# A hybrid attention and recurrence block on one core: where the position tables, the gate weights and two heads' weights stand in the instruction order

## The chip, the cores and the metric

One core of a Trainium2 chip runs the whole kernel. The time is that of the device for one execution, in microseconds (us): the median of three runs of the kernel before is 1267.96 us (1267.69 to 1269.3). Engines: PE multiplies matrices, DVE does elementwise work and scans, ACT does activations and copies, POOL elementwise work on the side, and SP issues the DMA transfers from one queue, in program order. Every engine carries out its instructions in the order in which they stand; it waits only when an operand is not there or a buffer is not free.

## The reference

The block has 2048 latent tokens of width 1024 and 256 context tokens. Only the parts that the change touches are shown: the biases of the windowed attention (`rpb`), the recurrence (RG-LRU) in two directions, and the heads' projections.

```python
q, k, v, z_a, u, z_l = jnp.split(h @ w, [aw, 2*aw, 3*aw, 4*aw, 4*aw + lw], axis=-1)
k_c, v_c = jnp.split(hc @ w[:, aw:3*aw], 2, axis=-1)
u_c = hc @ w[:, 4*aw:4*aw + lw]
attn = neighbourhood_attention(rope(qn), qn, rope(kn), v, kcn, vch, rpb)   # 8 heads x 64

uc, ucc = depthwise_conv(u, conv_w, conv_b), depthwise_conv(u_c, conv_w, conv_b)
for d, reverse in ((0, False), (1, True)):                 # 8 blocks x 64 channels
    r = sigmoid(u_block @ w_a[d] + b_a[d]); i = sigmoid(u_block @ w_x[d] + b_x[d])
    log_a = -8 * r * softplus(-lam[d])
    a, b = exp(log_a), sqrt(-expm1(2 * log_a)) * (i * u)
    h_t = a_t * h_prev + b_t                               # context first, then latent
y = forward + backward
mix = concat([attn * silu(z_a), y * silu(z_l)]) @ w_out
out = x + gate * mix
```

## The kernel before

Every projection of float32 data is made of three fp16 matmuls (high and low parts of activations and weights, lines 345 to 347 in `proj_ct`). A weight tile is loaded whole into `wraw`, its absolute maximum is found on DVE (L320) and brought to one value by PE and DVE (L112 to L117), and it is split into `wh` on ACT (L325) and `wl` on DVE (L326); this is `wsplit`.

Phase 1 norms the tokens, builds the position tables (`tables`), then projects and convolves the recurrence's input in four chunks of 128 channels (`u_proj(c)`: PE matmuls, an ACT copy `us` L363, DVE convolution L365 and L370). `gate` (L577) sums eight loaded rows of `w_mod` on DVE into `gacc` and closes with two matmuls on PE (L596).

For each chunk c, `lru` loads four 64x2x64 pieces of the recurrence's gate weights into `gw` (L424), after POOL has zeroed it (L421), and splits it on DVE into `gh` (L427) and `gl` (L428). For each direction d it multiplies them with `uh`, `ul` on PE (L448 to L450, called the gate matmuls here), takes tanh on ACT (L452) and works out the coefficients on ACT and DVE (L453 to L460); X is a (128 x 2304) and I its companion. Direction 0 is scanned on DVE at once (L462), direction 1 behind both (L469, three scans of 256, 1024 and 1024 steps); POOL adds the two (L472), and SP writes the chunk's result away. Between the directions `fill(d)` stands: two blocks of the silu gate (`z_units`, 24 matmuls a block, L480 on ACT and L481 on DVE) and, for d = 0, the weights of the next silu group (`z_group`). After chunk 0 and after chunk 1 the code writes `u_proj(2)` and `u_proj(3)`.

Three buffers matter. `gw` is one of two slots of the pool tag "z", which `us` (the convolution's copies) and `sz` (the silu gate's blocks) use as well, so a chunk's `gw` waits for the last `us` in front of it and the next `us` waits for `gw` to be read. Raw weights have one slot in each of two pools. In `tables` the source of constants `ng` stands in SBUF, in the tables' pool.

`tables` copies each quarter's table together on ACT (`te`, L665 to L668), sends it to DRAM (`d_t`), and copies it from there in 24 transfers (L675) and two fills (L677) to `d_e`, from which the attention loads its biases later. All of this is issued on SP.

Phase 2 begins with the weights of heads 0 and 1 (`wsplit`, lines 947 and 948), then `head_proj(0)`: projection (L604 to L606), norms, rotation on POOL (from L707), transposes by DMA and the first attention step. `lru_gate` (L975) loads its first weights `wraw` behind that, to be measured on DVE (L320).

Where the code gives the order only in part, a scheduler sets it: it merges the engines' instructions by its own times, within what buffers, program order of a stream and queues allow.

Of the kernel before, what the change touches and what calls it, by code (L numbers as in the profile page):

```python
# [7 lines left out]
F32 = mybir.dt.float32  # L8
# [51 lines left out]
class K:  # L60
# [351 lines left out]
    def lru(self, c, uc, p, fill):  # L412


        nc, a = self.nc, self.a
        N = CTX + S
        t = lambda x: p.tile([128, N], F32, tag=x, name=x, bufs=2)
        A, X = t("A"), t("X")
        gl = p.tile([128, 4, 128], F32R, tag="gl", name="gl", bufs=1)
        gw = self.zp.tile([128, 512], F32, tag="z", name="gw", bufs=2).rearrange("p (g c) -> p g c", g=4)  # L420
        nc.gpsimd.memset(gw, 0.0)  # L421
        for g, nm in enumerate(("lru_wa", "lru_wx")):
            for f in range(2):
                nc.sync.dma_start(gw[64 * f:64 * f + 64, 2 * g:2 * g + 2, 64 * f:64 * f + 64],  # L424
                                  a[nm][:, 2 * c + f].rearrange("d i j -> i d j"))
        gh = p.tile([128, 4, 128], F32R, tag="gh", name="gh", bufs=1)
        nc.vector.tensor_copy(gh, gw)  # L427
        nc.vector.tensor_tensor(gl, gw, gh.bitcast(F32), ALU.subtract)  # L428

        I = t("I")  # L430
        uh = p.tile([128, N], F32R, tag="uh", name="uh", bufs=1)
        ul = p.tile([128, N], F32R, tag="ul", name="ul", bufs=1)
        done = []
        for d in range(2):
            if d:
                A, X, I = t("A"), t("X"), t("I")
            kc = slice(4 * d + c, 4 * d + c + 1)
            for b in (0, CTX, CTX + 512, CTX + 1024, CTX + 1536):
                m = 512 if b else CTX
                s = slice(b, b + m)  # L440
                u = uc[:, s]
                if d == 0:
                    nc.scalar.copy(uh[:, s], u)  # L443
                    nc.gpsimd.tensor_tensor(ul[:, s], u, uh[:, s].bitcast(F32), ALU.subtract)  # L444
                for g, dst in enumerate((X, I)):
                    w = 2 * g + d
                    q = self.any_bank()[:, :m]
                    nc.tensor.matmul(q, gh[:, w, :], uh[:, s], start=True, stop=False)  # L448
                    nc.tensor.matmul(q, gh[:, w, :], ul[:, s], start=False, stop=False)
                    nc.tensor.matmul(q, gl[:, w, :], uh[:, s], start=False, stop=True)  # L450
                    k = 8 * g + 4 * d + c
                    nc.scalar.activation(dst[:, s], q, AF.Tanh, bias=self.hb[:, k:k + 1], scale=0.5)  # L452
                nc.vector.scalar_tensor_tensor(I[:, s], I[:, s], 1.0, u, ALU.add, ALU.mult)  # L453
            for h in range(2):
                s = slice(N // 2 * h, N // 2 * (h + 1))
                nc.scalar.activation(A[:, s], X[:, s], AF.Exp, bias=self.nk4[:, kc], scale=self.nk4[:, kc])
                nc.vector.scalar_tensor_tensor(I[:, s], A[:, s], 1.0, I[:, s], ALU.add, ALU.mult)
                nc.scalar.activation(X[:, s], X[:, s], AF.Tanh, bias=self.k2[:, kc], scale=self.k2[:, kc])
            nc.scalar.activation(X, X, AF.Sqrt, scale=0.25)
            nc.vector.tensor_tensor(X, X, I, ALU.mult)  # L460
            if d == 0:
                nc.vector.tensor_tensor_scan(A, A, X, 0.0, ALU.mult, ALU.add)  # L462
            done.append(A)
            fill(d)
        F, A = done
        init = 0.0
        for o, m in ((0, CTX), (CTX + S // 2, S // 2), (CTX, S // 2)):
            r = lambda x: x[:, o:o + m][:, ::-1]
            nc.vector.tensor_tensor_scan(r(A), r(A), r(X), init, ALU.mult, ALU.add)  # L469
            init = A[:, o:o + 1]  # L470
            if o:
                nc.gpsimd.tensor_tensor(F[:, o:o + m], A[:, o:o + m], F[:, o:o + m], ALU.add)  # L472
                nc.sync.dma_start(self.d_y[128 * c:128 * c + 128, o - CTX:o - CTX + m], F[:, o:o + m])
# [10 lines left out]
    def phase1(self, left, right):  # L484
# [14 lines left out]
        with ExitStack() as s1:  # L499
# [54 lines left out]
            with ExitStack() as s2:  # L554
                p = self.pool(s2, "lru")
                ug[2] = u_group(2)
                z_group()

                def z_units(c, d):
                    wh, wl, _ = za[c]  # L560
                    for tb in (2 * d, 2 * d + 1):
                        z = self.silu_z(self.zp, self.bank("mm"), wh, wl, self.zs[:, c:c + 1], tb)
                        dz = self.d_z[c][tb].rearrange("p (j f x) -> p f j x", j=4, f=2)
                        for f in range(2):
                            zf = z[:, 256 * f:256 * f + 256]
                            nc.sync.dma_start(dz[:, f, 0:3], zf[:, 32:224].rearrange("p (j x) -> p j x", j=3))
                            nc.sync.dma_start(dz[:, f, 3].rearrange("p (e x) -> p e x", e=2),
                                              bass.AP(zf.tensor, zf.offset, [list(zf.ap[0]), [224, 2], [1, 32]]))
                    if d == 0 and c < 3:
                        z_group()  # L570

                for c in range(4):
                    self.lru(c, ucs[c], p, lambda d, c=c: z_units(c, d))
                    if c < 2:
                        ucs.append(u_proj(c + 2))

# [32 lines left out]
    def tables(self, q):  # L609
# [26 lines left out]
        nc.sync.dma_start(d_r, rp)  # L636
        d_f = self.drm.tile([16, 2, NH, 15, 32], F32, name="d_f")
        ng = q.tile([128, 864], F32, name="ng")
        nc.gpsimd.memset(ng, NEG)
        ff = d_f.rearrange("q t h k c -> (q t h k c)").rearrange("(p n) -> p n", p=128)  # L640
        for i in range(2):
            nc.sync.dma_start(ff[:, 480 * i:480 * i + 480], ng[:, 0:480])
# [7 lines left out]
        for t in range(3):  # L650

            if t != 1:
                src = lambda k0, k1: d_f[:, t // 2, :, k0:k1, :].rearrange("q h k c -> h q (k c)")
                u = q.tile([128, 864], F32, tag="tu", name="tu")
                nc.gpsimd.memset(u, NEG)
                nc.sync.dma_start(u[:, 224:480], src(3, 11))
                w = q.tile([128, 480], F32, tag="tw", name="tw")
                nc.sync.dma_start(w, src(0, 15))
            for r in range(4):
                e = q.tile([128, 1024], F32, tag="te", name="te", bufs=2)  # L660
                for tab, o, g in ((u, 0, 5), (w, 640, 3)):
                    eo = e[:, o:o + 128 * g].rearrange("p (g c r) -> p g c r", c=32, r=4)
                    ti = tab[:, 96 - 32 * r:96 - 32 * r + 128 * g].rearrange("p (g r c) -> p g c r", r=4, c=32)
                    if t == 1:
                        nc.scalar.copy(eo[:, :, 0:16], ti[:, :, 16:32])  # L665
                        nc.scalar.copy(eo[:, :, 16:32], ti[:, :, 0:16])
                    else:
                        nc.scalar.copy(eo, ti)  # L668
                nc.sync.dma_start(d_t[r][t], e)

        self.d_e = [self.drm.tile([2, NH, 64, 3, w], F32, name=f"d_e{i}") for i, w in enumerate(BW)]

        def spread(rt, f, r, o, src, n):
            e = self.d_e[rt][f].rearrange("h (c r) t w -> (h c) r t w", r=4)[:, r, :, o:o + n]
            nc.sync.dma_start(e, d_t[r][:, :, src:src + n].rearrange("t p w -> p t w"))  # L675
        for f, o in ((0, 256), (1, 0)):
            nc.sync.dma_start(self.d_e[2 * f][f].rearrange("h (c r) t w -> (h c) (r t) w", r=4)[:, :, o:o + 128],  # L677
                              ng[:, 0:128].unsqueeze(1).broadcast_to([128, 12, 128]))
        for r in range(4):
            for f in range(2):  # L680
                spread(1, f, r, 0, 128 * (1 - f), 512)
            spread(0, 1, r, 0, 128, 384)
            spread(0, 0, r, 0, 768, 256)
            spread(2, 0, r, 0, 128, 384)
            spread(2, 1, r, 128, 640, 256)

    def bias_load(self, p, h, rt):

# [233 lines left out]
    def phase2(self, left, right):  # L922
# [5 lines left out]
        with ExitStack() as sg:  # L928
# [13 lines left out]
                nc.gpsimd.memset(x[:, :, 64:128], 0.0)  # L942
            self.zero = self.const.tile([128, 1], F32, name="zero")
            nc.gpsimd.memset(self.zero, 0.0)
            self.hw, self.bias, self.o = {}, [], {}
            with self.tc.issue_after(self.last.ins):
                for i in range(2):
                    self.hw[i] = self.wsplit(*self.head_w(i))
                for H in self.head_proj(0, p, q):
                    pass  # L950
            lz = self.lru_gate()
# [191 lines left out]
```

## Time and profile before

| | |
|---|---|
| median of three runs | 1267.96 us (1267.69 to 1269.3) |
| profiled execution | 1268.18 us |
| its span in the trace | 1266.4 us |
| mean granted TensorE clock | 0.945 |
| PE busy | 1116.4 us, 88% of the span |
| DVE, ACT, POOL busy | 926.4, 618.0 and 472.2 us |

A row of the trace gives the start and duration of an instruction, and in brackets the engine's idle time in front of it with what ended it. A matmul's duration overlaps the next one's, so the busy time of a stretch divided by its matmuls gives the pace. Three stretches are to be told apart: the recurrence's chunks (about 120 to 420 us of the span), the handoff to head 0 (to about 480), and the attention behind it.

### The profile page before, as it was taken

How to read it: one execution, taken by the hardware profiler on the slowest of the kernel's cores; microseconds unless marked ns; L12 is line 12 of the kernel's file. 1: busy time of each engine (PE TensorE's matmuls, PEld its weight loads, DVE VectorE, ACT ScalarE, POOL GpSimd, SP SyncE). 2: the span in 40 equal slices, each digit the busy share in tenths (PEclk: the TensorE clock that was granted, in tenths of full speed). 3: DMA queues.
4: the chain of work that ended last, by engine and by line, in shares of the span. 5: the costliest groups of instructions: out<-in, count | busy, mean ns of one | idle time of the engine just before them, and what ended most of it. 6: DMA issues, size and time to landing. Idle time of an engine off the chain costs nothing. (4 is left out here: it accounts for less than half of the span.)

```text
span 1266.4 us, 26204 instructions
## 1 busy us (share of the span) xinstructions
PE 1116.4 (88%) x9964; PEld 854.8 (67%) x9964; DVE 926.4 (73%) x2548; ACT 618.0 (49%) x1189; POOL 472.2 (37%) x861
## 2 busy tenths in 40 slices
PE   7767658996985959999999999999998997999997
PEld 1434324453543857899878988789887876888786
DVE  7898556869688667888978988788888874554432
ACT  1697118283588125655646555555555644231200
POOL 0245100403030377566564655646556462000000
PEclk9798869998998888999989999999999998999999
DMA  9746962111112623344533445335353537436352
GB/s 352 270 165 243 310 193 51 59 46 56 24 30 59 152 35 82 70 104 107 110 83 64 109 92 126 83 66 108 89 122 81 136 93 193 142 101 187 109 153 67
DMA packets 196014, 149.50 MB, mean 118 GB/s; under 512 B 129453, under 2 KB 168109, under 8 KB 195887
## 3 DMA queue, kind: packets, MB, share of 16 engines
q1 hardware_dynamic: 195887, 147.82, 43.6%
q8 instruction: 78, 1.28, 0.4%
q14 instruction: 49, 0.40, 0.1%
HBM read 96.42 MB, written 47.94 MB: 114 GB/s over the span
## 5 line engine op out<-in xcount | busy, mean ns | idle before, releaser
L604 PE MATMUL mm<-wh,hh 128*128 128x192 f16 x960 | 237.0, 247 | 1.7 <-DVE V L762 1.6
L605 PE MATMUL mm<-wl,hh 128*128 128x192 f16 x960 | 236.9, 247 | 0.0
L606 PE MATMUL mm<-wh,hl 128*128 128x192 f16 x960 | 236.9, 247 | 0.0
L895 DVE TENSOR_TENSOR Pl<-pt,Ph 128x384 f16<-128x384 f32 (+1 forms) x256 | 127.9, 517 | 57.2 <-ACT Ph L894 56.4
L345 PE MATMUL mm<-hh,wh 128*128 128x512 f16 x384 | 150.8, 393 | 17.9 <-DVE sz L481 12.0
L346 PE MATMUL mm<-hl,wh 128*128 128x512 f16 x384 | 150.0, 391 | 7.8 <-POOL hl L290 6.9
L887 ACT ACTIVATE SP<-SP,nb 128x640 f32<-128x640 f32 (+1 forms) x128 | 110.4, 880 | 94.2 <-DVE nb L885 89.8
L347 PE MATMUL mm<-hh,wl 128*128 128x512 f16 x384 | 148.7, 388 | 0.7 <-DVE wl L326 0.7
L894 ACT CAST Ph<-pt 128x384 f16<-128x384 f32 (+1 forms) x256 | 107.1, 452 | 79.2 <-PE pt L893 75.3
L893 PE MATMUL pt<-id,SP 128*128 128x128 f32 x704 | 116.9, 283 | 2.4 <-ACT SP L887 1.7
L604 PEld LDWEIGHTS <-hh 128*128 128x128 f16 x1024 | 100.6, 98 | 8.9 <-issue 5.2
L605 PEld LDWEIGHTS <-hh 128*128 128x128 f16 x1024 | 100.6, 98 | 2.8 <-issue 1.6
L606 PEld LDWEIGHTS <-hl 128*128 128x128 f16 x1024 | 100.5, 98 | 0.8
L882 DVE CUSTOM_DVE_ANT_0 SP<-sl,b,m 128x384 f32<-128x384 f32 (+1 forms) x128 | 93.4, 736 | 6.9 <-PE sl L830 6.2
L830 PE MATMUL sl<-qk,qt 128*128 128x128 f16 (+2 forms) x800 | 79.4, 232 | 17.9 <-DMA qk<-ST 8.2
L444 POOL TENSOR_TENSOR ul<-uc,uh 128x512 fp32r<-128x512 f32 (+1 forms) x20 | 30.5, 1553 | 151.0 <-ACT uh L443 150.9
L900 PEld LDWEIGHTS <-Ph 128*128 128x128 f16 x1408 | 79.5, 97 | 9.0 <-ACT Ph L894 2.9
L893 PEld LDWEIGHTS pt<-id,SP 128*128 128x128 f32 x704 | 79.4, 144 | 6.9 <-ACT SP L887 2.8
L346 PEld LDWEIGHTS <-wh 128*128 128x128 f16 x416 | 42.1, 101 | 59.2 <-issue 23.6
L347 PEld LDWEIGHTS <-wl 128*128 128x128 f16 x416 | 41.8, 101 | 56.9 <-issue 17.2
L719 POOL TENSOR_TENSOR ST<-P,ST 128x256 f16<-128x256 f32 x64 | 43.5, 680 | 93.7 <-ACT ST L718 93.4
L900 PEld LDWEIGHTS <-Pl 128*128 128x128 f16 x704 | 66.0, 99 | 17.1 <-DVE Pl L895 11.1
(303 smaller groups left out, 3049.5 us busy)
## 6 DMA issues: line engine op xcount, KB each, us to landing
b<-d_e SPq DMA_DIRECT2D x32, 288.0 KB
wm<-w_mod SPq DMA_DIRECT2D x16, 512.0 KB
x<-x SPq DMA_DIRECT2D x16, 512.0 KB
wraw<-w_in SPq DMA_DIRECT2D x12, 512.0 KB
d_t<-te SPq DMA_DIRECT2D x12, 512.0 KB
d_e<-d_t SPq DMA_DIRECT2D x8, 768.0 KB
wraw<-w_in SPq DMA_DIRECT2D x24, 256.0 KB
b<-d_e SPq DMA_DIRECT2D x16, 384.0 KB
```

The lines of the kernel that those rows point to most:

```text
L345: nc.tensor.matmul(out, wh[:, k, :], hh[:, k, :n], start=(k == 0), stop=False)
L346: nc.tensor.matmul(out, wh[:, k, :], hl[:, k, :n], start=False, stop=False)
L347: nc.tensor.matmul(out, wl[:, k, :], hh[:, k, :n], start=False, stop=(k == KC - 1))
L604: nc.tensor.matmul(out, hh[:, k, t0:t0 + 128], wh[:, k, :], start=(k == 0), stop=False)
L605: nc.tensor.matmul(out, hh[:, k, t0:t0 + 128], wl[:, k, :], start=False, stop=False)
L606: nc.tensor.matmul(out, hl[:, k, t0:t0 + 128], wh[:, k, :], start=False, stop=(k == KC - 1))
L882: nc.vector.tensor_tensor_reduce(SP[:, 0:W], sl[:, 0:W], bt[:, CT[j], 0:W], self.qs, m1, ALU.add, ALU.max, accum_out=m2)
L887: nc.scalar.activation(SP[:, :N], SP[:, :N], AF.Exp, bias=nb)
L893: nc.tensor.transpose(pt[:, i - c0, :], SP[:, 128 * i:128 * i + 128], self.id32)
L894: nc.scalar.copy(Ph[:, c0:c1], pt)
L895: nc.vector.tensor_tensor(Pl[:, c0:c1], pt, Ph[:, c0:c1], ALU.subtract)
L900: nc.tensor.matmul(pv[:, jj], P[:, i, :], v[:, w:w + 66], start=(i == j0 == 0), stop=(i == nch - 1 and j0 == 2))
```

## The change

Three things are moved. (1) The 26 transfers to `d_e` leave `tables` and become a generator of four parts, called between the directions of the recurrence's first three chunks; the two fills read their constants from a small DRAM tile instead of from SBUF. (2) `gw` gets a buffer of its own. (3) The weights of heads 0 and 1 are split in chunk 3's `fill` instead of at phase 2's beginning.

```diff
@@ lru
-        gw = self.zp.tile([128, 512], F32, tag="z", name="gw", bufs=2).rearrange("p (g c) -> p g c", g=4)
+        gw = p.tile([128, 4, 128], F32, tag="gw", name="gw", bufs=1)
@@ phase 1
+                self.hw = {}
+
+                spread = self.table_spread()
+
+                def fill(c, d):
+                    z_units(c, d)
+                    if (c, d) in ((0, 1), (1, 0), (1, 1), (2, 0)):
+                        next(spread)
+                    if c == 3:
+                        self.hw[d] = self.wsplit(*self.head_w(d))
+
                 for c in range(4):
-                    self.lru(c, ucs[c], p, lambda d, c=c: z_units(c, d))
+                    self.lru(c, ucs[c], p, lambda d, c=c: fill(c, d))
@@ tables
+        bneg = self.drm.tile([128, 128], F32, name="d_n")
         nc.gpsimd.memset(ng, NEG)
+        nc.sync.dma_start(bneg, ng[:, 0:128])
...
+        self.d_t, self.bneg = d_t, bneg
+
+    def table_spread(self):
+
+        nc, d_t = self.nc, self.d_t
         self.d_e = [...]
...
-                              ng[:, 0:128].unsqueeze(1).broadcast_to([128, 12, 128]))
+                              self.bneg.unsqueeze(1).broadcast_to([128, 12, 128]))
         for r in range(4):
...
             spread(2, 1, r, 128, 640, 256)
+            yield
@@ phase 2
-            self.hw, self.bias, self.o = {}, [], {}
+            self.bias, self.o = [], {}
             with self.tc.issue_after(self.last.ins):
-                for i in range(2):
-                    self.hw[i] = self.wsplit(*self.head_w(i))
                 for H in self.head_proj(0, p, q):
                     pass
```

The order on SP around chunk 0's gate weights, before. `d_e<-d_t` are the spreads, `wg` and `grow` belong to `gate`, the first `wraw` is the weight tile of the first silu group.

```order
52 L675 DMA d_e_1025<-d_t_958 128x3x256
53 L675 DMA d_e_1027<-d_t_958 128x3x384
54 L675 DMA d_e_1027<-d_t_958 128x3x256
55 L584 DMA wg<-w_mod 128x1024 x2
56 L593 DMA grow<-b_mod 1x1024
57 L424 DMA gw<-lru_wa 64x2x64 x2
58 L424 DMA gw<-lru_wx 64x2x64 x2
59 L312 DMA wraw<-w_in 128x8x128
60 L584 DMA wg<-w_mod 128x1024 x6
```

And now, on SP (the line numbers of the changed code are larger):

```order
43 L692 DMA d_e_1809<-d_t_958 128x3x384
44 L424 DMA gw<-lru_wa 64x2x64 x2
45 L424 DMA gw<-lru_wx 64x2x64 x2
46 L692 DMA d_e_1809<-d_t_958 128x3x256
...
51 L595 DMA wg<-w_mod 128x1024 x2
52 L604 DMA grow<-b_mod 1x1024
...
60 L692 DMA d_e_1811<-d_t_960 128x3x256
61 L424 DMA gw<-lru_wa 64x2x64 x2
62 L424 DMA gw<-lru_wx 64x2x64 x2
63 L312 DMA wraw<-w_in 128x8x128
64 L595 DMA wg<-w_mod 128x1024 x5
```

Chunk 0's `gw` moved in front of fifteen spreads, and chunk 1's `gw` in front of the silu group's `wraw`. The spreads did not move: all 24 stand in front of that `wraw`, as before.

The order on DVE where chunk 1 begins, before: the end of `u_proj(2)`, then `gh` and the first coefficients.

```order
345 L370 SCALAR_TENSOR_TENSOR uc<-cy_1975,cw_1499,uc 128x1
346 L370 SCALAR_TENSOR_TENSOR uc<-us,cw_1499,uc 128x511
347 L370 SCALAR_TENSOR_TENSOR uc<-us,cw_1499,uc 128x512 x2
348 L427 CAST gh<-gw 128x512
349 L428 TENSOR_TENSOR gl<-gw,gh 128x512
350 L481 SCALAR_TENSOR_TENSOR sz<-sz,mm 128x512
351 L453 SCALAR_TENSOR_TENSOR I<-I,uc 128x256
```

And now on DVE, the beginning and the end of the same `u_proj(2)`:

```order
313 L427 CAST gh<-gw 128x512
...
316 L428 TENSOR_TENSOR gl<-gw,gh 128x512
...
329 L453 SCALAR_TENSOR_TENSOR I<-I,uc 128x256
...
352 L457 SCALAR_TENSOR_TENSOR I<-A,I 128x1152
353 L370 SCALAR_TENSOR_TENSOR uc<-us,cw_1472,uc 128x512
354 L453 SCALAR_TENSOR_TENSOR I<-I,uc 128x512
355 L457 SCALAR_TENSOR_TENSOR I<-A,I 128x1152
356 L460 TENSOR_TENSOR X<-X,I 128x2304
```

`gh` moved from behind `u_proj(2)` to its front, and the first direction of chunk 1 (L453, L457, L460) now stands between its pieces. Both directions of chunk 2 stand in front of the end of `u_proj(3)` in the same way.

The order on PE where head 0 begins, before: the last gate matmuls of chunk 3, then the maximum of head 0's weights (L115), then the projection.

```order
2055 L448 MATMUL sc<-uh,gh 128x512
2056 L449 MATMUL sc<-ul,gh 128x512
2057 L450 MATMUL sc<-uh,gl 128x512
2058 L115 MATMUL mm<-av,id_63 128x1
2059 L604 LDWEIGHTS hhc
2060 L604 MATMUL sl<-wh,hhc 128x128
```

And now on PE, the last silu block of chunk 3 and head 0:

```order
2094 L346 MATMUL mm<-hl_109,wh 128x512
2095 L347 LDWEIGHTS wl
2096 L347 MATMUL mm<-hh_108,wl 128x512
2097 L615 LDWEIGHTS hhc
2098 L615 MATMUL sl<-wh,hhc 128x128
```

The maximum of head 0's weights left the place in front of the projection.

## Rows read from the trace of the kernel before

**Rows 1.** The page: span, and busy time of the engines.

```profile
span 1266.4 us, 26204 instructions
...
PE 1116.4 (88%) x9964; PEld 854.8 (67%) x9964; DVE 926.4 (73%) x2548; ACT 618.0 (49%) x1189; POOL 472.2 (37%) x861
```

**Rows 2.** Busy time by stretch, then granted clock, DMA share and GB/s.

```profile
core 0: us, PE busy (x) PEld busy (x) DVE busy (x) ACT busy (x) POOL busy (x), PEclk, DMA share, GB/s
...
148.50:168.60 20.10, 0.02 (x1) 0.00 (x0) 7.05 (x17) 1.59 (x3) 0.00 (x0) 0.58 0.92 294
...
240.00:256.00 16.00, 14.50 (x68) 6.33 (x65) 13.45 (x20) 3.26 (x6) 6.35 (x3) 1.00 0.20 74
256.00:311.00 55.00, 43.48 (x196) 24.92 (x197) 42.79 (x49) 37.06 (x46) 10.22 (x6) 0.88 0.16 39
311.00:328.00 17.00, 15.28 (x72) 6.93 (x71) 15.02 (x26) 1.94 (x6) 2.87 (x2) 1.00 0.18 69
328.00:373.00 45.00, 39.55 (x180) 22.05 (x179) 33.14 (x35) 38.60 (x46) 9.03 (x6) 0.96 0.13 27
...
480.00:1266.00 786.00, 751.36 (x8015) 645.06 (x8013) 570.04 (x1880) 364.01 (x821) 341.91 (x691) 0.98 0.44 108
```

**Rows 3.** Timeline of SP's queue: start, duration, line, transfer, count.

```profile
117.96 36.56 SPq L675 DMA_DIRECT2D d_e<-d_t  x19
...
158.07 2.39 SPq L424 DMA_DIRECT2D gw<-lru_wa  x2
160.51 3.06 SPq L424 DMA_DIRECT2D gw<-lru_wx  x2
...
164.06 0.40 SPq L312 DMA_DIRECT2D wraw<-w_in  x1
```

**Rows 4.** Timeline of PE, end of the longest gap (idle before, releaser).

```profile
168.64 0.58 PE L448 MATMUL sl<-uh,gh 128*128 128x256 f32 x1 [20.12 <-DVE gh L427]
...
178.58 0.39 PE L345 MATMUL mm<-hh,wh 128*128 128x512 f16 x1 [1.67 <-ACT wh L325]
```

**Rows 5.** Timeline of DVE, and one row of POOL: chunks 0 to 3.

```profile
168.16 0.42 DVE L427 CAST gh<-gw 128x512 fp32r<-128x512 f32 x1
...
169.23 1.21 DVE L320 TENSOR_REDUCE wm<-wraw 128x1 f32<-128x1024 f32 x1
...
179.36 1.28 DVE L326 SCALAR_TENSOR_TENSOR wl<-wraw,ws,wh 128x1024 f16<-128x1024 f32 x1
...
255.91 0.43 DVE L427 CAST gh<-gw 128x512 fp32r<-128x512 f32 x1 [2.34 <-DMA gw<-lru_wx]
...
276.12 2.56 DVE L460 TENSOR_TENSOR X<-X,I 128x2304 f32<-128x2304 f32 x1 [2.01 <-ACT X L459]
...
307.96 4.34 DVE L469 TENSOR_TENSOR_SCAN A<-A,X 128x1024 f32<-128x1024 f32 x1
...
377.69 4.46 DVE L469 TENSOR_TENSOR_SCAN A<-A,X 128x1024 f32<-128x1024 f32 x1
...
377.34 2.66 POOL L472 TENSOR_TENSOR A<-A 128x1024 f32<-128x1024 f32 x1 [9.33 <-DVE A L469]
...
417.46 2.35 DVE L469 TENSOR_TENSOR_SCAN A<-A,X 128x1024 f32<-128x1024 f32 x1
```

**Rows 6.** Timeline of ACT: first tanh of chunk 3.

```profile
373.63 0.48 ACT L452 ACTIVATE X<-sl,hb 128x256 f32<-128x256 f32 x1 [2.42 <-PE sl L450]
```

**Rows 7.** Timeline of PE: head 0 begins.

```profile
411.50 0.26 PE L604 MATMUL sl<-wh,hhc 128*128 128x128 f16 x1 [4.50 <-ACT wh L325]
...
414.49 0.26 PE L605 MATMUL sl<-wl,hhc 128*128 128x128 f16 x1 [2.56 <-DVE wl L326]
```

**Rows 8.** Timeline of DVE, SP and POOL: the handoff.

```profile
441.38 1.22 DVE L320 TENSOR_REDUCE wm<-wraw 128x1 f32<-128x1024 f32 x1 [7.95 <-DMA wraw<-w_in]
...
432.77 0.79 SPq L312 DMA_DIRECT2D wraw<-w_in  x1
...
445.78 1.18 POOL L707 TENSOR_TENSOR P<-rg,qrs 128x256 f32<-128x256 f32 x2 [10.79 <-DVE rq L93]
```

## The prediction, made before the changed kernel was run

> **What bounds the kernel now.** I read the page first [rows 1]: PE is busy for 88% of a span of 1266.4 us, so the question is where the other 12% lies. The busy time by stretch answers it [rows 2]. From 480 to 1266 us, the attention, PE works 751.36 of 786 us: that part is PE's own, and the change puts nothing into it. Ahead of it no engine is full. From 148.5 to 168.6 all four are nearly idle while the transfers take 0.92 of the DMA engines' time. From 240 on the chunks come in two kinds by turns: a convolution stretch, where DVE works 13.45 of 16 us and ACT 3.26, and a recurrence stretch of 55 us where ACT works 37.06 and DVE 42.79; then the same again (15.02 of 17 on DVE, and 38.60 of 45 on ACT). The two kinds want different engines and stand one behind the other. Then I read the timelines at the seams: the queue of SP [rows 3], the end of PE's longest gap [rows 4], DVE through the chunks [rows 5], ACT at chunk 3 [rows 6], and the handoff to head 0 [rows 7, 8].
>
> The chain that I follow is therefore: chunk 0, chunk 1, chunk 2, chunk 3, the last scan on DVE, head 0's projection and rotation, the first attention step. What ends earlier there moves everything behind it by as much.
>
> **Chunk 0 and the 20 us gap.** PE waits 20.12 us for `gh` [rows 4], which waits for `gw`, issued at 158.07 and 160.51 behind nineteen spreads that hold the queue for 36.56 us [rows 3]. In the new order `gw` stands in front of fifteen of them, so `gh` moves forward by some 20 us, to about 145, and chunk 0's first 24 gate matmuls with it. But these are only the first part of what follows. PE's next work is the first silu group, which begins at 178.58 after waiting for its split weights [rows 4]; DVE measures these (L320) at 169.23 [rows 5], 5.2 us after the tile was issued at 164.06 [rows 3]. In the new order that transfer still stands behind all 24 spreads and also behind eight `gw` transfers. Saved is what `gw` took between spreads and `wraw`, nothing, since the same transfers still precede it; lost are four more of them, 2.39 + 3.06 us at the throttled pace of rows 3 or nothing where the DMA is free. PE's order then holds the silu group's 40 matmuls and `gate`'s two closing ones in front of the rest of chunk 0. So chunk 0 ends as before: I take 0, with bounds of -20.1 (the whole gap is gained) and +5.5 (the four transfers).
>
> The Trainium skill, page "DMA: Bandwidth & Descriptors", section "Queues, rings and completion order", says that SP's copies go to its own rings and that each DMA engine takes up descriptors in ring order. By it the first silu group's tile cannot overtake the spreads, and the gain in the gap is 0; a queue without that order would give up to 20 us. The rows agree: the tile is used only after the spreads have drained.
>
> **Chunk 1 beside `u_proj(2)`.** `gh` comes at 255.91 now, behind the convolution and 2.34 us of waiting for `gw`, and the first direction's coefficients are complete (L460) at 276.12 [rows 5]. In the new order `gh` is in front of `u_proj(2)` and the five L453 and two L457 of that direction stand inside it; the last piece of the convolution and L460 are neighbours. The DVE work so inserted is some 6 us: L453 and L457 each go once over the 2304 columns that L460 goes over in 2.56 us [rows 5], so 5.1 us, and some overhead for their seven pieces (the stretch of rows 2 has 16 - 13.45 = 2.55 us of idle DVE to take a part). ACT, with 3.26 of 16 us there, has the room for its tanh. The convolution ends at 255.91 - 2.34 = 253.6 now, so L460 comes at about 253.6 + 6 = 260 instead of 276.12: 16 us earlier. The rest of the chunk, to the end of its last scan (307.96 + 4.34 = 312.3), keeps its length or gains a little: it ends at about 294 to 296, 16 to 18 earlier.
>
> **Chunks 2 and 3.** In the new order both directions of chunk 2 stand in front of the end of `u_proj(3)`. The stretch that it fills is ACT's: 38.60 us of work [rows 2], with a start-up gap as chunk 3's 2.42 [rows 6]. From 294 that gives a last scan ending at about 335, where it now ends at 377.69 + 4.46 = 382.15. That looks like 47 us, but most of it is an exchange: what stood between is now behind. Four silu blocks of chunk 2 now stand back to back in front of chunk 3, and the weights of the group are split behind the scans. A block is 24 matmuls at 14.50 us by 68, 0.213 us each [rows 2], so 5.1 us, four are 20.4. Chunk 3's first tanh then comes at 335 + 1.3 (the split, L326 [rows 5]) + 20.4 + 2.4 + 1.2 (the last block's two evacuations of 512 columns, 0.6 each at the pace of L460) = 360.3, say 361, instead of 373.63 [rows 6]: 12.6 earlier. Chunk 3 took 417.46 + 2.35 - 373.63 = 46.2 us. It no longer carries chunk 2's three scans on DVE (4.46, 2.35 for one of the same length without POOL, and some 0.6 for 256 steps: 7.4 us), and takes on the heads' weights (two L320 and one L326 in front of the last scan, 1536 columns each, so 1.5 times the 1.21 and 1.28 of rows 5: 5.5 us): 44 us. The last scan ends at 405 instead of 419.8, 15 earlier.
>
> **The handoff.** Head 0's projection waits 4.50 us for `wh` and 2.56 for `wl` [rows 7]; the weights are split earlier now, so it begins when chunk 3's last silu block is done, about 396 by the same 15 us. What counts is what the rotation on POOL waits for: it begins at 445.78, behind DVE's wait of 7.95 us for a `wraw` issued only at 432.77 [rows 8], 8.6 us from issue to use. That transfer now stands in front of the rotation table, the bias loads and the transpose, right behind the chunk's result. I take half of the 7.95 as gained, 4 us, with bounds of 0 and 7.95; PE's two waits are beside this path and I add nothing for them (bound 2.56).
>
> **The sum.** 0 (gap) - 15 (chunks) - 4 (handoff) = -19. The profiled execution took 1268.18 us, its span 1266.4, and the median of the runs is 1267.96, so the difference between them is small: 1268 - 19 = 1249 us. The fills read from DRAM instead of SBUF and cost one more small transfer; they are two of 26 in a queue that later loads wait for only in the attention, so nothing. POOL's zeroing of `gw` moves forward where POOL is idle (2.87 of 17 us busy in the convolution stretch [rows 2]). The likeliest case's own range is 1241 (chunks -18, handoff -8, and PE's 1) to 1258 (chunks -10, no gain in the handoff).
>
> **The rivals.**
>
> *The gap is gained as well.* If the silu group's tile lands early, chunk 0 ends 20.1 us earlier and so do all chunks behind it: 1249 - 20 = 1229 us. For it: nothing but `gh` is named as releaser [rows 4]. Against: the tile's place in SP's queue and the order on PE. Chance 0.09.
>
> *The interleaving gives nothing.* DVE is full enough in the convolution stretch, and it slows beside POOL: chunk 2's third scan takes 4.46 us while POOL adds from 377.34 for 2.66 us, against 2.35 for the same scan in chunk 3 [rows 5]. If about eight of the interleaved DVE operations pay such 2.1 us, some 15 us of gain are gone and only the handoff's 4 stay: 1264 us. Against: POOL does little in these stretches (6.35 of 16, 2.87 of 17 [rows 2]). Chance 0.12. The Trainium skill, page "SBUF — State Buffer", section "Who interferes with whom", says that a DVE instruction with two inputs in SBUF contends with a GpSimd instruction that reads SBUF and that the later one waits. The scan agrees: it ends 2.15 us after POOL's add does.
>
> *The order does not do what the words say.* The spreads do not move beside the recurrence: all 24 are still in front of the first silu group's tile. If the chunks are bound by something else that did not move (the silu blocks on PE, the spreads), the time stays: 1266 to 1270. Against: in the stretches from 240 to 328 DVE and ACT take turns. Chance 0.08.
>
> *Slower: chunk 2 in front of `u_proj(3)`.* The convolution was hidden between the chunks' ends; put behind chunk 2 it becomes serial, and so do four silu blocks. If nothing of `u_proj(3)` runs beside chunk 2, chunk 3's first tanh comes not at 361 but at 335 + 17 [rows 2] + 1.3 + 4 x 7.9 (a block with its evacuation waited out, 5.1 + 1.2 and as much again for the two engines' answer, 1.6) + 4 = 389, the last scan at 433, 13 later than now, less 4 for the handoff: 1277 us. It decides from where the first tanh comes later than about 380 (419.8 + 4 - 44). For it: only two buffers hold silu blocks. Against: PE and DVE are free enough beside ACT's 38.6 of 45 us. Chance 0.09.
>
> **How the numbers follow.** The likeliest case has 0.62. A difference under 0.2%, 2.5 us, can't be told from no change. Faster: 0.62 + 0.09 + 0.12 = 0.83; same 0.08; slower 0.09. The range from 1236 to 1267 holds the likeliest case but for its far tail, the third case and the near half of no change, and leaves out the full gain of the gap and the slower case.
>
> **What would show it.** Right: `gh` of chunk 0 near 145 and a PE gap that stays, now ended by `wh` of the first silu group; chunk 1's first L460 near 260; chunk 2's last scan near 335; chunk 3's first tanh near 361; the last scan near 405; head 0's L604 (now L615) at about 396 without a wait for `wh`; the first rotation on POOL near 425; the wait for `wraw` under 4 us; the attention as long as before. Wrong: the silu group's weights in use before 170 (the gap is gained), L460 of chunk 1 after 270, or chunk 3's first tanh after 375.

## The result, and the profile after

The changed kernel takes 1247.53 us (median of four runs, 1246.06 to 1250.8) against 1267.83 before; the ratio is 0.9839 with a 95% interval of 0.9812 to 0.9865. That is 20 us faster, where 19 were forecast. The profiled execution took 1246.92 us with a span of 1245.1, which is 21.3 shorter than before. Where these 21.3 us lie is read from the same rows as before, one seam after another.

First SP's queue and PE in front of chunk 0, which answer to [rows 3, 4]. Columns as there: start, duration, line (those of the changed code are larger), instruction, count, and in brackets the idle time in front with its releaser.

```profile
126.63 1.82 SPq L424 DMA_DIRECT2D gw<-lru_wa  x2
...
143.71 17.41 SPq L692 DMA_DIRECT2D d_e<-d_t  x9
...
165.74 0.40 SPq L312 DMA_DIRECT2D wraw<-w_in  x1
```

```profile
172.54 0.59 PE L112 MATMUL po<-id,wm 128*1 128x128 f32 x2 [21.73 <-DVE wm L320]
...
177.16 0.61 PE L345 MATMUL mm<-hh,wh 128*128 128x512 f16 x1 [2.43 <-ACT wh L325]
...
190.23 1.02 PE L607 MATMUL pt<-gacc,gone 128*1 128x512 f32 x2
...
192.03 0.38 PE L448 MATMUL pt<-uh,gh 128*128 128x256 f32 x1
```

The gate weights left at 126.63 instead of 158.07, in front of fifteen spreads. The weights of the first silu group (`wraw`) left at 165.74, later than the 164.06 of before, and PE's gap is 21.73 us, where it was 20.12: only its releaser has another name. Next stand the silu blocks from 177.16 on (178.58 before) and `gate`'s closing matmuls at 190.23 (190.06 before); the chunk's other 36 gate matmuls are behind these, from 192.03 on, among more silu matmuls and those of `u_proj(2)`.

Then DVE through the chunks, and ACT at the beginning of chunk 3, answering to [rows 5, 6].

```profile
139.76 0.43 DVE L427 CAST gh<-gw 128x512 fp32r<-128x512 f32 x1 [1.52 <-DMA gw<-lru_wx]
...
171.27 1.22 DVE L320 TENSOR_REDUCE wm<-wraw 128x1 f32<-128x1024 f32 x1 [15.55 <-DMA wraw<-w_in]
...
186.39 1.29 DVE L600 SCALAR_TENSOR_TENSOR gacc<-wg,silu,gacc 128x1024 f32<-128x1024 f32 x1
...
260.54 2.56 DVE L460 TENSOR_TENSOR X<-X,I 128x2304 f32<-128x2304 f32 x1 [0.52 <-ACT X L459]
...
297.74 2.34 DVE L469 TENSOR_TENSOR_SCAN A<-A,X 128x1024 f32<-128x1024 f32 x1
...
338.33 2.33 DVE L469 TENSOR_TENSOR_SCAN A<-A,X 128x1024 f32<-128x1024 f32 x1
...
403.99 5.44 DVE L469 TENSOR_TENSOR_SCAN A<-A,X 128x256 f32<-128x256 f32 x3
```

```profile
364.80 0.69 ACT L480 ACTIVATE sz<-mm,zs 128x512 f32<-128x512 f32 x1 [4.75 <-PE mm L347]
365.38 0.47 ACT L452 ACTIVATE I<-pt,hb 128x256 f32<-128x256 f32 x1
```

`gh` of chunk 0 comes at 139.76 (168.16 before) and nothing follows from it; `gate`'s last sum on DVE ends at 187.7, shortly before its closing matmuls on PE; L460 of chunk 1 comes at 260.54 (276.12). The last scans of chunks 1 and 2 end at 300.1 and 340.7 (312.3 and 382.15), but of chunk 3's tanh only the first stands early, at 353.62, and the others run from 365.38 on (373.63 for the first before), behind a silu block that ACT waited 4.75 us for: PE is working through the blocks that now stand together. The last scan ends at 409.4 (419.8).

The busy time of the two kinds of stretch, answering to [rows 2] and with its columns, and of the attention, taken here from its first matmul that waits for a transposed tile (455.8; 474.9 before) to the end:

```profile
240.00:256.00 16.00, 16.00 (x75) 8.46 (x74) 15.82 (x24) 9.44 (x15) 3.44 (x2) 1.00 0.16 66
256.00:311.00 55.00, 47.37 (x225) 29.01 (x224) 50.60 (x56) 44.67 (x58) 13.95 (x8) 0.97 0.22 61
455.80:1245.10 789.30, 751.04 (x8042) 643.90 (x8041) 572.80 (x1893) 365.94 (x827) 347.69 (x702) 0.99 0.44 107
```

From 240 to 256 ACT now works 9.44 us where it worked 3.26, and DVE and PE are full; in the next 55 us DVE's share is 50.60 (42.79). The attention's 789.3 us are 791.5 before.

And the handoff, answering to [rows 7, 8]:

```profile
397.71 0.22 PE L615 MATMUL sl<-wh,hhc 128*128 128x128 f16 x1
...
414.26 1.81 DVE L326 SCALAR_TENSOR_TENSOR wl<-wraw,ws,wh 128x1536 f16<-128x1536 f32 x1
415.99 0.28 DVE L789 TENSOR_TENSOR rgc<-sl,gs 128x128 f32<-128x128 f32 x1
...
419.92 1.22 DVE L320 TENSOR_REDUCE wm<-wraw 128x1 f32<-128x1024 f32 x1 [2.14 <-DMA wraw<-w_in]
...
416.10 0.38 SPq L312 DMA_DIRECT2D wraw<-w_in  x1
...
426.85 1.18 POOL L725 TENSOR_TENSOR P<-rg,qrs 128x256 f32<-128x256 f32 x2 [0.18 <-DVE qrs L95]
```

PE begins head 0 at 397.71 without idle time (411.50). DVE takes up head 0's first results at 415.99, behind the last scan and without a wait for PE; it waits 2.14 us for the first weights behind it (7.95), and POOL's rotation begins at 426.85: 18.9 earlier than 445.78. The attention's first such matmul is 19.1 earlier, and 2.2 more are gained in the attention.

### The profile page after: what moved, and what is told of

Same layout as the page of the kernel before. It is cut to its first block, busy times and chain, and to the rows that moved or that the text cites. A ratio compares the mean times of both kernels' runs of the same rounds, so it can differ in the third digit from the quotient of the medians.

```text
span 1245.1 us, 26214 instructions
## 1 busy us (share of the span) xinstructions
PE 1108.7 (89%) x9964; PEld 848.7 (68%) x9964; DVE 926.8 (74%) x2548; ACT 615.4 (49%) x1187; POOL 469.7 (38%) x861
## 3 DMA queue, kind: packets, MB, share of 16 engines
q8 instruction: 78, 1.28, 0.4%
```

## The experiments

The theory was: the own buffer of `gw` carries the chunks' part of the gain, the heads' weights the handoff's, the spreads nothing, because they still stand in front of the first silu group's weights. Its rivals: the spreads in four parts carry the gain, the parts work only together, or the gain is all in the handoff. Each kernel was timed in five rounds against the kernel before.

### E1: the own buffer alone

The kernel before with one line changed:

```diff
-        gw = self.zp.tile([128, 512], F32, tag="z", name="gw", bufs=2).rearrange("p (g c) -> p g c", g=4)
+        gw = p.tile([128, 4, 128], F32, tag="gw", name="gw", bufs=1)
```

> The kernel before, with only the gate weights' own buffer. Theory: the own buffer is what lets the scheduler put the gate weights' split in front of the convolution and so lay chunk 1 and 2 beside it; it carries the 15 us of the chunks: 1268 - 15 = 1253 us, first L460 of chunk 1 near 260, last scan on DVE near 405, while head 0's projection still waits for its weights. Rival 1 (the gain needs the spreads in four parts): 1266 to 1269. Rival 2 (the gain is of the handoff alone): 1266 to 1269.

Measured: 1252.8 us, ratio 0.9882 (0.9859 to 0.9905). DVE, PE and POOL of its trace:

```profile
166.88 0.42 DVE L427 CAST gh<-gw 128x512 fp32r<-128x512 f32 x1
...
256.45 2.56 DVE L460 TENSOR_TENSOR X<-X,I 128x2304 f32<-128x2304 f32 x1
...
399.68 2.35 DVE L469 TENSOR_TENSOR_SCAN A<-A,X 128x1024 f32<-128x1024 f32 x1
...
403.92 0.27 PE L604 MATMUL sl<-wh,hhc 128*128 128x128 f16 x1 [7.43 <-ACT wh L325]
...
414.09 0.29 DVE L771 TENSOR_TENSOR rgc<-sl,gs 128x128 f32<-128x128 f32 x1 [5.63 <-ACT sqc L769]
...
436.00 1.18 POOL L707 TENSOR_TENSOR P<-rg,qrs 128x256 f32<-128x256 f32 x2 [2.05 <-DVE rq L93]
```

`gh` of chunk 0 is not earlier at all (166.88), but L460 of chunk 1 is (256.45), and the last scan ends at 402.0, even 7 earlier than in the full change. Both rivals are out. What the rows also show: head 0's projection waits 7.43 us for its weights, more than the 4.50 of before, and DVE, done with the last scan, waits 5.63 us for head 0's first results. Of 17.8 us gained at the last scan, 9.8 are left at the rotation. The profiled execution's other 7 or so lie behind the rotation and were not traced to a place.

### E2: the heads' weights alone

```diff
-                    self.lru(c, ucs[c], p, lambda d, c=c: z_units(c, d))
+                    self.lru(c, ucs[c], p, lambda d, c=c: fill(c, d))   # fill: z_units, and wsplit(head_w(d)) at c == 3
...
-                for i in range(2):
-                    self.hw[i] = self.wsplit(*self.head_w(i))
```

> The kernel before, with only the split of heads 0 and 1 moved into chunk 3. Theory: only the handoff gains, 4 to 7 us: 1261 to 1264 us; last scan on DVE at about 420 as before, the wait of 7.95 us for the first weights of the silu group behind it shrinks to 2 to 4, and head 0 begins without the waits of 4.50 and 2.56 us. Rival (the split's 5.5 us on DVE push the last scan back by as much): 1267 to 1270.

Measured: 1253.33 us, ratio 0.9886 (0.9863 to 0.991): 14 us, twice the upper end of what was expected. The traced execution is the slowest of the six, 9.9 us below the traced one of before.

```profile
418.81 4.43 DVE L469 TENSOR_TENSOR_SCAN A<-A,X 128x1024 f32<-128x1024 f32 x1
...
423.58 1.21 DVE L320 TENSOR_REDUCE wm<-wraw 128x1 f32<-128x1024 f32 x1
...
397.89 0.26 PE L611 MATMUL mm<-wh,hh 128*128 128x192 f16 x1
...
433.54 1.19 POOL L714 TENSOR_TENSOR P<-rg,qrs 128x256 f32<-128x256 f32 x2 [0.64 <-DVE qrs L95]
```

The last scan ends at 423.2, 3.4 later than before: it starts 1.35 later, behind the split, and itself takes 4.43 us instead of 2.35. Still the kernel is faster, and the rotation begins 12.2 us earlier. That does not take the last scan off the path. From its end to the rotation DVE's rows show no idle time at all here, where before it stood idle for 10.3 of 26.0 us, 7.95 of them waiting for the next weights. What the move took away lies behind the scan: head 1's split now stands in front of it, and DVE finds the next weights without waiting at 423.58, so that 10.3 us are left between the scan and the rotation. PE begins head 0 at 397.89 instead of 411.50, but DVE takes up its results only behind the scan.

### E3: the spreads alone

```diff
-        (24 spreads and two fills issued in tables)
+        self.d_t, self.bneg = d_t, bneg      # table_spread(): four parts, next(spread) in fill
```

> The kernel before, with only the spreads as a generator of four parts and the fills read from DRAM. Theory: the scheduler issues all 24 spreads where they stood, in front of the first silu group's weights, so nothing changes: 1266.5 to 1269.5 us, the gap on PE at 148 to 168 stays 20 us. Rival (the four parts free SP's queue and carry part of the gain): 1255 to 1264.

Measured: 1264.67 us, ratio 0.9976 (0.9957 to 0.9994).

```profile
169.67 0.58 PE L448 MATMUL sl<-uh,gh 128*128 128x256 f32 x1 [23.68 <-DVE gh L427]
```

The gap on PE is still there, 23.68 us. The median lies 0.24% lower, just clear of no change, while the profiled execution took 1267.54 us; no row shows where 3 us would come from, and E5 asks again.

### E5: both other parts, without the spreads

E1 and E2 together.

> The changed kernel without its first part: the spreads as before, with the gate weights' own buffer and the heads' weights split in chunk 3. Theory: the two parts carry all of the gain, and overlap in the handoff, so their sum (14.6 + 14.1 us alone) is not reached: 1246 to 1250 us. Rival 1 (the spreads in four parts carry the 3 us that they showed alone): 1250 to 1253. Rival 2 (the spreads moved chunk 0's gate weights forward, and that is where some of the gain is): 1253 or more.

Measured: 1245.93 us, ratio 0.9825 (0.9805 to 0.9846), against 0.9839 (0.9812 to 0.9865) for the whole change: the same.

```profile
169.11 0.58 PE L448 MATMUL sl<-uh,gh 128*128 128x256 f32 x1 [20.41 <-DVE gh L427]
...
426.88 1.18 POOL L714 TENSOR_TENSOR P<-rg,qrs 128x256 f32<-128x256 f32 x2 [0.18 <-DVE qrs L95]
```

PE's gap of 20.41 us ends with `gh` of chunk 0 at 169.11, as before; the rotation begins at 426.88, as in the full change (426.85). So the first part of the change adds nothing on top of the other two, and the gate weights moved forward in chunk 0 are worth nothing. What E3 alone showed is not seen again. The two parts overlap: 14.6 and 14.1 us alone, 21.3 together, which fits the rows: E1's kernel stands waiting for the weights that E2 moves, and E2's for a chunk that E1 moves.

### E4: the spreads really beside the recurrence

The changed kernel, with each part held on SP behind the last weight load written in front of it:

```diff
-            self.nc.sync.dma_start(raw[:, :, o:o + w], wv[:, :, c:c + w])
+            self.wld = self.nc.sync.dma_start(raw[:, :, o:o + w], wv[:, :, c:c + w])
...
                     if (c, d) in ((0, 1), (1, 0), (1, 1), (2, 0)):
-                        next(spread)
+                        with self.tc.issue_after(self.wld.ins):
+                            next(spread)
```

> The changed kernel, with each of the four parts of the spreads held on SP behind the last weight load written in front of it, so that they really are issued beside the recurrence. Theory: the gap of 21.7 us on PE is the transfer of the first silu group's weights behind the spreads; with the spreads behind it, it is issued at about 149 instead of 165.7, as soon as the one raw slot is free, DVE measures it near 155 instead of 171, and all that follows comes 15 us earlier: about 1232 us. Rival 1 (gate's eight rows, which stand in front of it, take the place of the spreads): 1240 to 1248. Rival 2 (the spreads beside the recurrence hold up its small transfers on the same queue): 1250 or more, with waits of DVE for gw in chunks 1 to 3.

Measured: 1208.0 us, ratio 0.9528 (0.9502 to 0.9554). Faster than the change by 40 us, where 15 were expected. SP, DVE, PE and POOL:

```profile
137.61 0.59 SPq L312 DMA_DIRECT2D wraw<-w_in  x1
...
143.06 1.22 DVE L320 TENSOR_REDUCE wm<-wraw 128x1 f32<-128x1024 f32 x1 [0.42 <-DMA wraw<-w_in]
...
170.48 2.56 DVE L460 TENSOR_TENSOR X<-X,I 128x2304 f32<-128x2304 f32 x1 [2.36 <-ACT X L459]
...
149.14 1.02 PE L608 MATMUL pt<-gacc,gone 128*1 128x512 f32 x2 [0.55 <-DVE gacc L601]
...
150.94 0.38 PE L448 MATMUL pt<-uh,gh 128*128 128x256 f32 x1
...
161.63 0.39 PE L345 MATMUL mm<-hh,wh 128*128 128x512 f16 x1
...
388.61 1.18 POOL L726 TENSOR_TENSOR P<-rg,qrs 128x256 f32<-128x256 f32 x2 [0.18 <-DVE qrs L95]
```

The silu group's tile leaves at 137.61 instead of 165.74, within 0.7 us of its slot becoming free, and is measured at 143.06 instead of 171.27: 28.2 us. The other 12.2 come behind it: from the measuring to L460 of chunk 0 it is 27.4 us here and 39.6 in the change (171.27 to 210.91). PE carries out 39 of the chunk's 60 gate matmuls from 150.94 to 161.6, and only then begins the silu blocks (nine gate matmuls come later); in the changed kernel the first silu matmuls, from 177.16 on, stand in front. So from the measuring to the first gate matmul behind `gate`'s closing ones (150.94 and 192.03) it is 7.9 us here and 20.8 in the change, and from there to L460 about the same (19.5 and 18.9). All that follows keeps this lead: the rotation begins at 388.61, 38.2 earlier.

The held spreads let a second load forward, the rows of `gate`. Its closing matmuls, which stand in front of these gate matmuls in both kernels, come at 149.14 instead of 190.23, and PE waits 0.55 us for their sums and not for the tile. L460 follows them by 21.3 us here and by 20.7 in the change. So the place of the spreads is what counts; how much of it goes through the tile and how much through `gate`'s rows no run parts.

The busy time by stretch (PE, weight loads, DVE, ACT, POOL, granted clock, DMA share, GB/s):

```profile
150.00:170.00 20.00, 18.12 (x80) 10.28 (x79) 16.52 (x32) 18.37 (x24) 0.00 (x0) 1.00 0.46 113
170.00:190.00 20.00, 18.98 (x90) 10.01 (x87) 18.23 (x18) 18.98 (x22) 8.29 (x6) 1.00 0.82 242
```

From 170 to 190 the spreads take the DMA engines to a share of 0.82, and PE (18.98 of 20 us) and DVE (18.23) stay full beside them.

### E6: half of the spreads held

```diff
+                        if (c, d) in ((1, 1), (2, 0)):       # the other two parts: as in the change
                             with self.tc.issue_after(self.wld.ins):
                                 next(spread)
```

> The changed kernel with only the third and fourth part of the spreads held on SP behind the weight loads written in front of them; twelve spreads and both fills stay in front of the first silu group's weights. Theory: what chunk 0 waits for is the place of that tile behind the spreads, and then the silu blocks that PE has in front of the chunk's gate matmuls. With half the spreads away the tile is issued when the raw slot is free, near 147, so it lands near 153 instead of 171, and chunk 0's first L460 comes at 180 to 190 instead of 211: 1218 to 1228 us, between the change (1247.5) and all parts held (1208). Rival (only a queue without any spreads helps): 1240 or more.

Measured: 1229.15 us, ratio 0.9693 (0.967 to 0.9715), 1 us above what was expected and between the two.

```profile
151.95 0.38 SPq L312 DMA_DIRECT2D wraw<-w_in  x1
...
150.65 1.28 DVE L326 SCALAR_TENSOR_TENSOR wl<-wraw,ws,wh 128x1024 f16<-128x1024 f32 x1
...
165.55 1.86 PE L611 MATMUL pt<-gacc,gone 128*1 128x512 f32 x2
...
187.67 2.56 DVE L460 TENSOR_TENSOR X<-X,I 128x2304 f32<-128x2304 f32 x1 [2.41 <-ACT X L459]
```

The tile leaves at 151.95, as soon as its slot is free (150.65 + 1.28), so the twelve spreads in front no longer hold it back; it is measured at 156.20. `gate`'s closing matmuls come at 165.55, and L460 at 187.67, 22.1 behind them: about half the way from 210.91 to 170.48. That the half is due to the half of the spreads is not shown, since the tile waited for its slot.

### E7: the held spreads on the kernel before

E4's edit on the kernel before (in E3's form); gate weights and heads' weights as before.

> The kernel before, with the spreads in four parts held on SP behind the weight loads written in front of them; gate weights in the shared buffer and the heads' weights as before. Theory: the spreads' place is worth most of its 40 us without the two other parts: gh of chunk 0 comes near 153 (its shared slot is free after the convolution's last copy), first L460 near 185 instead of 211, and the chunks and the handoff then run as before: 1235 to 1246 us. Rival (without its own buffer chunk 0 still waits for gw, and nothing is gained): 1260 to 1268.

Measured: 1235.89 us, ratio 0.9756 (0.9735 to 0.9777).

```profile
159.59 0.43 DVE L427 CAST gh<-gw 128x512 fp32r<-128x512 f32 x1 [0.78 <-DMA gw<-lru_wx]
...
181.39 2.56 DVE L460 TENSOR_TENSOR X<-X,I 128x2304 f32<-128x2304 f32 x1 [3.19 <-ACT X L459]
```

L460 of chunk 0 comes at 181.39 (210.75 before), 29.4 earlier, and the kernel is 31 us faster. Here chunk 0 waits for its own gate weights: `gh` comes at 159.59, after `gate`'s closing matmuls (148.65). `gh` of chunk 1 still waits behind the convolution (232.21). So the place of the spreads is worth more by itself than the three parts of the change.

### E8: the spreads held, but all at one place

E4 with all four parts issued in chunk 0's second `fill`.

```diff
-                    if (c, d) in ((0, 1), (1, 0), (1, 1), (2, 0)):
+                    if (c, d) == (0, 1):
                         with self.tc.issue_after(self.wld.ins):
-                            next(spread)
+                            for _ in spread:
+                                pass
```

> The changed kernel with all four parts of the spreads issued at one place, held behind the second silu group's weight load. Theory: it is the queue in front of chunk 0 that counts, not the four parts, and the DMA engines have room in the recurrence: 1206 to 1214 us, as with the parts apart (1208). Rival (a solid block of 24 transfers holds up the gate weights, the next weights and the results that stand behind it on the same queue): 1218 or more, with waits of DVE for gw or wraw of 10 us around 200.

Measured: 1217.98 us, ratio 0.9611 (0.9591 to 0.963): 10 us slower than E4, on the rival's side. SP, ACT and PE:

```profile
165.94 22.32 SPq L694 DMA_DIRECT2D d_e<-d_t  x12
...
198.09 12.57 SPq L694 DMA_DIRECT2D d_e<-d_t  x10
210.75 2.05 SPq L424 DMA_DIRECT2D gw<-lru_wa  x2
...
197.44 0.69 ACT L480 ACTIVATE sz<-mm,zs 128x512 f32<-128x512 f32 x1 [3.63 <-DMA d_z<-sz]
...
224.00 0.55 PE L448 MATMUL sl<-uh,gh 128*128 128x256 f32 x1 [4.48 <-DVE gh L427]
```

Chunk 2's gate weights leave SP behind the last of the spreads, at 210.75, and PE waits 4.48 us for their split; ACT waits 3.63 us for the transfer that empties a silu buffer, which stands behind the first twelve spreads. The waits are shorter than the 10 us that the rival named, and of PE and ACT, not of DVE. That the four parts matter once they are held is shown; that these two waits make the 10 us is not. At the first L460 of chunk 2 the kernel is only 1.6 us behind E4 (284.74 against 283.19), at the end of that chunk's last scan 12.6 (316.6 against 304.0): the loss appears there, where the scheduler's order differs as well, and its cause stays open.

## Why the prediction was right, point by point

*The gap in front of chunk 0.* Right: the gap stays, and E5 shows that `gh` earlier is worth nothing. The reason given, the tile's place behind the spreads in SP's queue, is right as far as the spreads go (E4, E6, E7): in the change the tile's slot is free at 148.2 and it leaves at 165.74. But `gate`'s rows stood behind the same spreads, and its closing matmuls at 190.23 held the rest of the chunk as much; no run moves the tile without the rows. And the upper bound was wrong. I priced the whole gap at 20.1 us; removing it is worth 40 with the other two parts and 31 without, since the rows named one idle stretch and not the price of the silu and closing matmuls that stood behind it and in front of the chunk.

*Chunk 1 beside the convolution.* Right in mechanism, and in size at the first L460: 260.54 for a forecast of 260, and E1 alone gives 14.6 us. The chunk's last scan ends at 300.1 and not at 294 to 296.

*Chunks 2 and 3.* Right in kind: 41 us earlier at the end of chunk 2 shrink to 8 at chunk 3's beginning, because the silu blocks now stand in between. Chunk 2 ends at 340.7 (335 forecast), chunk 3's first tanh comes at 353.6, but the next only at 365.4 (361 forecast), and the last scan ends at 409.4 (405): 10.4 earlier where I had 15. The slower rival's point was 380, so it was not near. "The interleaving gives nothing" fell as well: the third scans of chunks 1 and 2 take 2.34 and 2.33 us now, not 4.34 and 4.46 [rows 5].

*The handoff.* The path was right, and both sizes on it were off, in opposite directions. The rotation follows the last scan, on DVE, over the work and the waits that stand between them:

| kernel | last scan ends | rotation begins | between them | of it DVE idle |
|---|---|---|---|---|
| before | 419.8 | 445.78 | 26.0 | 10.3 |
| E1 | 402.0 | 436.00 | 34.0 | 11.6 |
| E2 | 423.2 | 433.54 | 10.3 | none |
| changed | 409.4 | 426.85 | 17.4 | 2.1 |
| E4 | 371.1 | 388.61 | 17.5 | 2.2 |

So the 18.9 us are 10.4 at the last scan, where I had 15, and 8.5 behind it, where I had 4. That the sum came out is luck: two misses of some 4.5 us cancel. The handoff's term was too small because it took half of the wait of 7.95 us, which shrank by 5.8, and left out DVE's four shorter waits behind the scan, 2.3 us together, which are gone. PE's two waits at head 0 are beside the path, as I had it: in the changed kernel PE begins head 0 13.8 us earlier, and its results lie until DVE comes to them at 415.99. In E1, where head 0 begins late, they are on it (5.63 us).

The wait for `wraw` shrank as forecast (under 4: 2.14), and its place on SP fits as the reason. It leaves at 416.10, when the split of head 1's weights ends on DVE and frees the raw slot (414.26 + 1.81), and is used 3.8 us later. Before, it left at 432.77, 2.2 us after that split's end, behind the bias loads and a transpose, and was used 8.6 us later. That it can't leave before its slot is free is read from these times; no kernel with a second slot was run.

*The spreads.* Right: they did not move, and E5 is as fast without them. The fills from DRAM cost nothing that shows.

The Trainium skill says that on each DMA engine descriptors are consumed in ring order ("DMA: Bandwidth & Descriptors", "Queues, rings and completion order"). No run here tests that rule: the tile waits in front of its issue on SP, and from the issue to its use it is 5.5 us both in the change, behind all the spreads, and in E4, in front of them.

## What to carry to other kernels

A gap's length is not what its removal is worth: look at what the engine does right after it, in which order, whether the late load also decides that order, and which other loads stand behind the same transfers. In a handoff, price what stands on the path's own engine between the last step of one stage and the first of the next, work and every wait; a kernel that is faster although that last step comes later (E2) does not take the step off the path. And where work is said to run beside other work, look up its place in the queue: here the words were true only after an explicit edge held the transfers back, and that edge was worth twice the rest of the change.

## What was not expected of the hardware

The granted clock of the changed kernel, to be set beside E4's above (same columns):

```profile
150.00:170.00 20.00, 0.82 (x3) 0.33 (x3) 2.12 (x3) 0.00 (x0) 0.00 (x0) 0.60 0.97 318
170.00:190.00 20.00, 13.02 (x44) 5.05 (x44) 13.04 (x18) 1.83 (x2) 0.00 (x0) 0.63 0.56 182
```

PE's clock was 0.60 of full speed, near its lower level of 1.2 GHz, on the mean of the 20 us in which it stood still, and 0.63 in the next 20, in which it worked 13.02 us. In E4 both stretches have 1.00, the 2.4 GHz level. The silu blocks behind the gap ran in that slower stretch: 40 matmuls from 177.16 to 190.1, less 0.99 us of waiting, are 0.30 us each against 0.213 [rows 2], some 3.5 us in all. They stand 0.43 us apart at first and 0.22 from 184.7 on.
